# Batched 64x64 matmul: a second quarter of the last four a tiles loaded as fp32 on ScalarE's queue

## Chip, cores and metric

The kernel runs on one core of a Trainium2 chip. The metric is the device time of one execution in microseconds, as a median of runs. A core has five engines, each with its own queue of instructions: TensorE (PE; PEld is its weight load), VectorE (DVE), ScalarE (ACT), GpSimd (POOL) and SyncE (SP). DMAs are issued from the queues of SyncE, ScalarE and GpSimd, and all are carried by the same 16 DMA engines. In the profile q0 is GpSimd's DMA ring, q1 SyncE's and q10 ScalarE's.

## The reference

1024 independent products of 64x64 matrices in fp32:

```python
"a": np.random.randn(1024, 64, 64).astype(np.float32)
"b": np.random.randn(1024, 64, 64).astype(np.float32)

def reference(a, b):
    return np.matmul(a, b).astype(np.float32)
```

a and b are 16.8 MB each, and so is the output.

## The kernel before

**Tiling.** b and the output are cut into 16 tiles of 64 products (index t, 1 MB each), a into 8 tiles of 128 products (index s, 2 MB each); tile s of a serves t = 2s and 2s + 1. The multiplication is done in bf16: for each tile t TensorE runs 64 pairs of weight load and matmul, with a block-diagonal weight tile (`at_bd`) that holds transposed blocks of a, and `b_bf` as the moving data.

**a.** A tile of a is loaded in four quarters h = 0 to 3 of 512 KB (128 rows of 4 KB). For s = 1 to 7 `load_a` (line 70) has GpSimd load h = 0, 1, 2 with DMAs that cast from fp32 to bf16 on the way (256 KB written, tile `a_sb`), and SyncE load h = 3 as it is (fp32, tile `a_raw`). Tile 0 (`load_first_a`) is all fp32, two quarters from SyncE and two from ScalarE, each into a borrowed output buffer. Both tiles come from `a_pool`, three buffers each, so the load of tile s + 3 needs the buffer of tile s free. Load 4 is issued in the round t = 0, loads 5, 6 and 7 in the rounds t = 2, 4 and 6.

There are two ways from a to its transposed form `at_sb`. For s = 1, 2, 3 (`ON_DVE`) `transpose_dve` (line 116) has ScalarE cast h = 3 to bf16 (line 126) and VectorE transpose each quarter (line 128). For s = 0 and s = 4 to 7 `regroup` (line 100) brings the quarters into one tile `a_bf` in the order v, h, k on VectorE: line 109 copies the three cast quarters, line 112 casts and copies the fourth; then `transpose` (line 133) lets TensorE transpose and ScalarE copy the result from PSUM (line 141). `spread` (lines 154 and 164, VectorE) puts `at_sb` into the block-diagonal tile, of which there are two.

**b.** `load_b` (line 94) loads tile t as fp32, 512 rows of 2 KB, from SyncE where t is even and from ScalarE where t is odd. Three buffers: b(t + 3) is issued when the cast of b(t) has freed its buffer. `cast` (line 173) turns it into bf16 on VectorE (tile 0 on ScalarE; the last tile is shared by both, lines 178 and 180).

**Output.** `multiply` (line 187) runs the matmuls in two halves, each evacuated from PSUM in four copies (line 206). ScalarE does them all up to t = 6; from then on VectorE takes two of the last four in odd t. The stores of t = 0 to 13 are issued by GpSimd, 1 MB each, one round after the tile (`HOLD`), and those of the last two tiles by SyncE and ScalarE in halves and quarters (line 195).

**Order.** The order of the calls in the main loop is each engine's order (`manual_schedule`). In a round t: spread(t+1) and cast(t+1), load_b(t+3), load_a where it is due, the second half of a transposition, multiply(t), then the work on a for s + 2, and the store of t - 1. A DMA issue that waits holds up what stands behind it on its queue. On ScalarE that is the evacuation of tile t, on GpSimd the next store.

Of the kernel before, what the change touches and what calls it, by code (L numbers as in the profile page):

```python
# [8 lines left out]
fp32 = mybir.dt.float32  # L9
bf16 = mybir.dt.bfloat16  # L10
# [3 lines left out]
def kernel(  # L14
# [14 lines left out]
    nc = tc.nc  # L29
# [7 lines left out]
    N_BD = 2  # L37
    HOLD = 2
    ON_DVE = (1, 2, 3)

    a_v = a.rearrange("(s g h) (mp v) k -> s h g mp (v k)", h=4, g=32, v=16)
    b_v = b.rearrange("(t g h) (kp u) n -> t (h kp) g (u n)", h=4, g=16, u=2)
# [3 lines left out]
    a_pool = ctx.enter_context(tc.tile_pool(name="a_pool", bufs=A_AHEAD))  # L46
# [15 lines left out]
    a_tiles, b_tiles, abf_tiles, at_tiles, bbf_tiles = {}, {}, {}, {}, {}  # L62
# [6 lines left out]

    def load_a(s):  # L70

        a_sb = a_pool.tile([128, 3, 16, 64], bf16, name="a_sb")
        for h in range(3):
            nc.gpsimd.dma_start(  # L74
                out=a_sb[:, h, :, :].rearrange("p v k -> p (v k)"), in_=a_v[s, h], single_packet=True
            )
        a_raw = a_pool.tile([128, 16, 64], fp32, name="a_raw")
        nc.sync.dma_start(out=a_raw[:].rearrange("p v k -> p (v k)"), in_=a_v[s, 3])
        a_tiles[s] = a_sb, a_raw

    def load_first_a():

# [17 lines left out]
    def regroup(s):  # L100
        a_sb = a_tiles.pop(s)
        a_bf = work.tile([128, 16, 4, 64], bf16, name="a_bf")
        if s == 0:
            for h in range(4):
                copy = nc.scalar.copy if h % 2 else nc.vector.tensor_copy
                copy(a_bf[:, :, h, :], a_sb[h].rearrange("p (v k) -> p v k", v=16))  # L106
        else:
            cast_sb, raw = a_sb
            nc.vector.tensor_copy(  # L109
                a_bf[:, :, 0:3, :], cast_sb[:].rearrange("p h v k -> p v h k")  # L110
            )
            nc.vector.tensor_copy(a_bf[:, :, 3, :], raw[:])  # L112
        abf_tiles[s] = a_bf
        at_tiles[s] = work.tile([128, 32, 4, 4, 4], fp32, name="at_sb")

    def transpose_dve(s, half):
        cast_sb, raw = a_tiles[s]
        if half == 0:
            at_tiles[s] = work.tile([128, 4, 8, 4, 4, 4], fp32, name="at_sb")
        for h in (2 * half, 2 * half + 1):  # L120
            rows = cast_sb[:, h, :, :] if h < 3 else None
            if h == 3:
                rows = work.tile([128, 16, 4, 64], bf16, name="a_bf")[:, 0:4, :, :].rearrange(
                    "p x y k -> p (x y) k"
                )
                nc.scalar.copy(rows, raw[:])  # L126
            pairs = rows.rearrange("p v k -> p (v k)").bitcast(fp32)
            nc.vector.transpose(  # L128
                at_tiles[s][:, h].rearrange("p g w mp vo -> p w vo g mp"),
                pairs.rearrange("p (vo w kp) -> p w vo kp", vo=4, w=4),  # L130
            )

    def transpose(s, j):
        a_cols = abf_tiles[s][:].rearrange("p v h k -> p v (h k)").bitcast(fp32)
        for wl in range(2):
            at_ps = t_psum.tile([128, 4, 128], fp32, name="at_ps")
            for vo in range(4):
                nc.tensor.transpose(  # L138
                    at_ps[:, vo, :], a_cols[:, 4 * vo + 2 * j + wl, :], identity[:]
                )  # L140
            nc.scalar.copy(  # L141
                at_tiles[s][:, :, 2 * j + wl, :, :],
                at_ps[:].rearrange("p vo (g mp) -> p g mp vo", mp=4),
            )

    def spread(t):
        bd = bd_tiles[t % N_BD]
        at_sb = at_tiles[t // 2]
        for h in range(4):
            rows = slice(32 * h, 32 * h + 32)  # L150
            if t // 2 in ON_DVE:
                for i in range(2):
# [34 lines left out]
    def multiply(t):  # L187
# [20 lines left out]
        for half in range(2):  # L208
# [19 lines left out]
            if not last:  # L228
                copies = [nc.scalar.copy] * 4
                if half and t % 2 and t > 2 * max(ON_DVE):  # L230
                    copies[2:] = [nc.vector.tensor_copy] * 2
# [7 lines left out]
    with tc.manual_schedule():  # L239
# [7 lines left out]
        make_identity(nc, identity)  # L247
        nc.gpsimd.memset(bd_tiles[1][:, 0:8], 0.0)
        load_a(1)
        load_b(2)  # L250
        nc.gpsimd.memset(bd_tiles[1][:, 8:16], 0.0)
        load_a(2)
        regroup(0)
        transpose(0, 0)
        transpose(0, 1)
        spread(0)
        cast(0)
        for t in range(n_t):
            s, half = t // 2, t % 2
            if t + 1 < n_t:  # L260
                spread(t + 1)
                cast(t + 1)
            if t + B_AHEAD < n_t:
                load_b(t + B_AHEAD)
            if half == 0 and 0 < s < n_s - 1 - A_AHEAD:
                load_a(s + 1 + A_AHEAD)
            if half == 0 and 0 < s < n_s - 1 and s + 1 not in ON_DVE:
                transpose(s + 1, 1)
            multiply(t)
            if t == 0:  # L270
                transpose_dve(1, 0)
                transpose_dve(1, 1)
                a_tiles.pop(1)
                load_a(A_AHEAD)
                load_a(A_AHEAD + 1)
            if t and s + 2 in ON_DVE and (half or s):
                for part in [0, 1] if t == 1 else [half]:
                    transpose_dve(s + 2, part)
                if half:
                    a_tiles.pop(s + 2)  # L280
            elif half == 0 and 0 < s and s + 2 < n_s:
                regroup(s + 2)
            elif half == 1 and s + 2 < n_s:
                transpose(s + 2, 0)
            if t >= HOLD - 1:
                store(t - HOLD + 1)
# [32 lines left out]
```

## Time and profile before

| what | value |
|---|---|
| median of 3 runs | 133.84 us (133.62 to 133.94) |
| profiled execution | 133.61 us |
| its span, first to last instruction | 131.8 us |
| DVE busy | 101.8 us (77%) |
| ACT busy | 88.1 us (67%) |
| PE busy | 59.6 us (45%) |
| POOL busy | 31.9 us (24%) |
| granted TensorE clock | 0.763 |
| casting quarter of a (GpSimd), issue to landing | 15.9 us, median of 21 |
| fp32 quarter of a (SyncE), issue to landing | 17.3 us, median of 7 |
| VectorE waiting for b, whole span | 4.9 us in 3 waits, the longest 2.0 |

The profile is one execution. Busy time is what an engine spent in instructions other than issuing DMAs; a share of the span says nothing yet about what limits the end, since another engine's work or a transfer may have ended last at each step. The chain of waits follows the last instruction back through what released it. The DMA view counts packets and bytes of each ring and the time that the packets took as a share of 16 engines; a casting load's bytes are counted as written, half of what was read.

### The profile page before, as it was taken

What the parts mean: (1) busy time and instruction counts of PE and PEld (TensorE: products, weight loads), DVE (VectorE), ACT (ScalarE), POOL (GpSimd) and SP (SyncE); (2) the same over time, 40 slices, a digit from 0 to 9 for tenths busy, and PEclk for the clock granted to TensorE, in tenths of its full rate; (3) what the DMA queues carried; (4) which work ended last, traced back from release to release, by engine and by line L of the source; (5) the groups of instructions that cost most, each with busy time, mean ns of one, the idle gap of its engine ahead of it and who ended that gap; (6) DMA issues with size and microseconds to landing.
All of it is one profiled execution on the core that took longest, in us unless ns stands there. A gap on an engine that the chain in (4) does not pass through costs nothing.

```text
span 131.8 us, 2750 instructions
## 1 busy us (share of the span) xinstructions
PE 59.6 (45%) x1104; PEld 56.7 (43%) x1104; DVE 101.8 (77%) x144; ACT 88.1 (67%) x158; POOL 31.9 (24%) x43
## 2 busy tenths in 40 slices
PE   0006405730550640908662883299369619465000
PEld 0006305730550630908552872298368618464000
DVE  5930399529999984999999998699999997898300
ACT  2125414999495096492999989469969996549920
POOL 8991000340054000618031204300420302040000
PEclk9999975798568555595999599558968975579855
DMA  3999999999999999999999999999999999999993
GB/s 68 372 334 313 306 313 280 280 311 321 327 299 400 362 306 297 393 393 400 321 285 357 403 395 362 308 299 385 395 391 393 390 390 397 399 395 406 390 383 136
DMA packets 19020, 44.99 MB, mean 341 GB/s; under 512 B 1088, under 2 KB 3136, under 8 KB 19008
## 3 DMA queue, kind: packets, MB, share of 16 engines
q0 software_dynamic: 6832, 20.19, 50.6%
q1 hardware_dynamic: 7120, 14.68, 30.7%
q10 hardware_dynamic: 5056, 9.96, 20.1%
q8 instruction: 8, 0.13, 0.4%
q14 instruction: 4, 0.03, 0.1%
HBM read 33.55 MB, written 16.78 MB: 382 GB/s over the span
## 4 chain that ended last, share of the span: by engine, by line
DMA 53%; ACT 15%; DVE 14%; PE 6%; issue 5%; SPq 2%; ACTq 0%; DVEq 0%
DMA b_sb<-in_b_dram 53%; ACT o_sb L206 12%; PE o_ps L218 6%; DVE at_bd L164 4%; DVE b_bf L173 4%; DVE at_bd L154 2%; ACT b_bf L173 1%; DVE at_sb L128 1%; DVE o_sb L206 1%; DVE a_bf L109 1%; SPq L91 1%; ACT a_bf L126 1%; SPq L97 1%; ACT b_bf L180 1%; DVE a_bf L112 0%
## 5 line engine op out<-in xcount | busy, mean ns | idle before, releaser
L206 ACT COPY o_sb<-o_ps 64x512 f32<-64x512 f32 x112 | 65.0, 581 | 17.9 <-PE o_ps L218 13.5
L218 PEld LDWEIGHTS <-at_bd 128*128 128x128 bf16 x1024 | 45.2, 117 | 52.6 <-DVE b_bf L173 40.5
L218 PE MATMUL o_ps<-b_bf,at_bd 128*128 128x64 bf16 x960 | 45.6, 223 | 48.7 <-DVE b_bf L173 35.0
L164 DVE COPY at_bd<-at_sb 32x1024 f32<-32x1024 f32 x40 | 29.6, 739 | 6.6 <-ACT at_sb L141 5.6
L195 POOL DMA_DIRECT2D out_dram<-o_sb x14 | 15.4, 1103 | 46.1 <-ACT at_sb L141 20.6
L154 DVE COPY at_bd<-at_sb 32x512 f32<-32x512 f32 x48 | 22.0, 457 | 1.1
L74 POOL DMA_DIRECT2D a_sb<-in_a_dram x21 | 12.4, 606 | 38.5 <-DVE at_sb L128 33.2
L173 DVE CAST b_bf<-b_sb 128x2048 bf16<-128x2048 f32 x14 | 17.2, 1227 | 5.2 <-DMA b_sb<-in_b_dram 4.9
L138 PE MATMUL at_ps<-identity,a_bf 128*128 128x128 f32 x80 | 12.9, 329 | 11.0 <-ACT a_bf L106 11.0
L138 PEld LDWEIGHTS at_ps<-identity,a_bf 128*128 128x128 f32 x80 | 11.7, 176 | 11.0 <-issue 11.0
L141 ACT COPY at_sb<-at_ps 128x512 f32<-128x512 f32 x20 | 10.8, 591 | 2.7 <-PE at_ps L138 2.0
L128 DVE STREAM_TRANSPOSE at_sb<-a_sb 128x512 f32<-128x512 f32 x9 | 8.9, 1065 | 0.0
L128 DVE STREAM_TRANSPOSE at_sb<-a_bf 128x512 f32<-128x512 f32 x3 | 3.1, 1049 | 4.0 <-ACT a_bf L126 4.0
L206 DVE COPY o_sb<-o_ps 64x512 f32<-64x512 f32 x8 | 5.5, 690 | 0.2
L106 ACT CAST a_bf<-o_sb 128x1024 bf16<-128x1024 f32 x2 | 2.1, 1045 | 5.0 <-DMA o_sb<-in_a_dram 5.0
L173 ACT CAST b_bf<-b_sb 128x2048 bf16<-128x2048 f32 x1 | 1.9, 1897 | 4.0 <-DMA b_sb<-in_b_dram 4.0
L126 ACT CAST a_bf<-a_raw 128x1024 bf16<-128x1024 f32 x3 | 3.1, 1046 | 1.7 <-DMA a_raw<-in_a_dram 1.7
L109 DVE COPY a_bf<-a_sb 128x3072 bf16<-128x3072 bf16 x4 | 4.2, 1045 | 0.0
L106 DVE CAST a_bf<-o_sb 128x1024 bf16<-128x1024 f32 x2 | 2.8, 1383 | 1.8 <-DMA o_sb<-in_a_dram 1.8
L246 DVE MEMSET at_bd<- 128x4096 f32 x1 | 3.5, 3472 | 0.8 <-issue 0.8
L206 DVE COPY o_sb<-at_ps 64x256 f32<-64x256 f32 x8 | 3.4, 422 | 0.5 <-PE at_ps L218 0.4
L180 ACT CAST b_bf<-b_sb 128x512 bf16<-128x512 f32 x2 | 1.1, 616 | 3.5 <-DMA b_sb<-in_b_dram 3.5
(16 smaller groups left out, 15.4 us busy)
## 6 DMA issues: line engine op xcount, KB each, us to landing
out_dram<-o_sb POOLq DMA_DIRECT2D x14, 1024.0 KB, 22.7
a_sb<-in_a_dram POOLq DMA_DIRECT2D x21, 256.0 KB, 15.9
a_raw<-in_a_dram SPq DMA_DIRECT2D x7, 512.0 KB, 17.3
o_sb<-in_a_dram SPq DMA_DIRECT2D x2, 512.0 KB, 5.9
o_sb<-in_a_dram ACTq DMA_DIRECT2D x2, 512.0 KB, 7.0
out_dram<-o_sb SPq DMA_DIRECT2D x2, 512.0 KB, 5.5
out_dram<-o_sb SPq DMA_DIRECT2D x2, 256.0 KB, 5.2
out_dram<-o_sb ACTq DMA_DIRECT2D x2, 256.0 KB, 4.7
```

What stands on the lines that cost most here:

```text
L74: nc.gpsimd.dma_start(out=a_sb[:, h, :, :].rearrange("p v k -> p (v k)"), in_=a_v[s, h], single_packet=True)
L106: copy(a_bf[:, :, h, :], a_sb[h].rearrange("p (v k) -> p v k", v=16))
L109: nc.vector.tensor_copy(a_bf[:, :, 0:3, :], cast_sb[:].rearrange("p h v k -> p v h k"))
L128: nc.vector.transpose(at_tiles[s][:, h].rearrange("p g w mp vo -> p w vo g mp"), pairs.rearrange("p (vo w kp) -> p w vo kp", vo=4, w=4),)
L138: nc.tensor.transpose(at_ps[:, vo, :], a_cols[:, 4 * vo + 2 * j + wl, :], identity[:])
L141: nc.scalar.copy(at_tiles[s][:, :, 2 * j + wl, :, :], at_ps[:].rearrange("p vo (g mp) -> p g mp vo", mp=4),)
L154: nc.vector.tensor_copy(bd[rows, 8 * i : 8 * i + 8, :, h, :, :].rearrange("p g w mp vo -> p (g w) (mp vo)"), at_sb[block : block + 32, h]. ...
L164: nc.vector.tensor_copy(bd[rows, :, :, h, :, :].rearrange("p g w mp vo -> p (g w) (mp vo)"), at_sb[rows, half].rearrange("p g w mp vo -> p ...
L173: (nc.vector.tensor_copy if t else nc.scalar.copy)(b_bf[:], b_sb[:])
L195: store_queue(t, lo).dma_start(out=o_v[t, :, lo : lo + n, :], in_=o_sb[:, lo : lo + n].rearrange("p gh j wl n -> p (gh j wl n)"),)
L206: copies[2 * par + wl](dst, src)
L218: nc.tensor.matmul(o_ps[:, gl, g % 2, j, :], at_bd[:, j, g, :, u], b_bf[:, g, 64 * u : 64 * u + 64], start=(u == 0), stop=(u == 1),)
```

## The change

`load_a` takes one tile of 12 KB per partition, `room`, in which the cast quarters stand first and the fp32 quarters behind them, so both kinds now share one buffer and come free together. For s = 4, 5, 6, 7 (`TWO_RAW`) GpSimd casts two quarters instead of three, and h = 2 is loaded as fp32 by ScalarE; h = 3 stays with SyncE. `regroup` then copies two quarters and casts two on VectorE. For s = 1, 2, 3 the same quarters are loaded on the same queues as before.

```diff
+    TWO_RAW = (4, 5, 6, 7)
...
-        a_sb = a_pool.tile([128, 3, 16, 64], bf16, name="a_sb")
-        for h in range(3):
-            nc.gpsimd.dma_start(
-                out=a_sb[:, h, :, :].rearrange("p v k -> p (v k)"), in_=a_v[s, h], single_packet=True
-            )
-        a_raw = a_pool.tile([128, 16, 64], fp32, name="a_raw")
-        nc.sync.dma_start(out=a_raw[:].rearrange("p v k -> p (v k)"), in_=a_v[s, 3])
-        a_tiles[s] = a_sb, a_raw
+        n_cast = 2 if s in TWO_RAW else 3
+        room = a_pool.tile([128, 6144], bf16, name="a_sb")
+        a_sb = room[:, 0 : 1024 * n_cast].rearrange("p (h x) -> p h x", h=n_cast)
+        raw = room[:, 1024 * n_cast : 1024 * n_cast + 2048 * (4 - n_cast)].bitcast(fp32)
+        raw = raw.rearrange("p (h x) -> p h x", h=4 - n_cast)
+        for h in range(n_cast):
+            nc.gpsimd.dma_start(out=a_sb[:, h, :], in_=a_v[s, h], single_packet=True)
+        for h in range(n_cast, 4):
+            (nc.sync if h == 3 else nc.scalar).dma_start(out=raw[:, h - n_cast, :], in_=a_v[s, h])
+        a_tiles[s] = (
+            a_sb.rearrange("p h (v k) -> p h v k", v=16),
+            raw.rearrange("p h (v k) -> p h v k", v=16),
+        )
...
             cast_sb, raw = a_sb
+            n_cast = 2 if s in TWO_RAW else 3
             nc.vector.tensor_copy(
-                a_bf[:, :, 0:3, :], cast_sb[:].rearrange("p h v k -> p v h k")
-            )
-            nc.vector.tensor_copy(a_bf[:, :, 3, :], raw[:])
+                a_bf[:, :, 0:n_cast, :], cast_sb.rearrange("p h v k -> p v h k")
+            )
+            nc.vector.tensor_copy(
+                a_bf[:, :, n_cast:4, :], raw.rearrange("p h v k -> p v h k")
+            )
...
-                nc.scalar.copy(rows, raw[:])
+                nc.scalar.copy(rows, raw[:, 0])
```

## The prediction

> **What bounds the kernel now.** I read the page's slices and DMA queues first, then the DMA queues window by window, then the chain of waits, then VectorE's and ScalarE's timelines.
>
> The page's slices (tenths of busy DMA engines) and its queues: q0 is GpSimd's ring, which carries the casting loads of a and the stores of t = 0 to 13; q1 is SyncE's and q10 ScalarE's.
>
> ```profile
> DMA  3999999999999999999999999999999999999993
> q0 software_dynamic: 6832, 20.19, 50.6%
> q1 hardware_dynamic: 7120, 14.68, 30.7%
> q10 hardware_dynamic: 5056, 9.96, 20.1%
> HBM read 33.55 MB, written 16.78 MB: 382 GB/s over the span
> ```
>
> The 16 DMA engines are full from slice 2 to slice 39, and the shares sum to 101%. So an edit that leaves the bytes read and written as they are can win only what the engines don't fill now. At the end that is little: in the table by stretches the DMA share is 1.08 in 126 to 128 us, 0.86 in 128 to 130 and 0.08 in 130 to 131.8, about 0.8 us of full work missing.
>
> How the rings share the engines is seen in three windows of the DMA queue view (packets, MB, share of 16 engines): 40 to 44 us, 51 to 56 us, and 32 to 38 us.
>
> ```profile
> q0 software_dynamic: 196, 0.78, 50.6%
> q10 hardware_dynamic: 196, 0.40, 26.8%
> q1 hardware_dynamic: 198, 0.41, 26.4%
> ```
> ```profile
> q0 software_dynamic: 336, 1.05, 66.4%
> q1 hardware_dynamic: 331, 0.72, 38.9%
> q10 hardware_dynamic: 1, 0.00, 0.0%
> ```
> ```profile
> q0 software_dynamic: 282, 0.51, 45.1%
> q1 hardware_dynamic: 279, 1.02, 44.7%
> q10 hardware_dynamic: 213, 0.40, 17.8%
> ```
>
> Each ring with work gets one packet in turn, whatever its size. With three rings SyncE's gets 198 packets in 4 us (50 per us); with ScalarE's ring empty it gets 331 in 5 us (66 per us). ScalarE's ring is empty in gaps: 37 to 39.5, 51 to 56.5, 67.5 to 70.5, 93 to 94.5 us in the trace's packet record, because an odd b is issued only when a buffer comes free and its first packet follows some 4 us later (issued 52.54, first packet 56.5; 66.47 and 70.5). SyncE's ring is not empty once between 39 and 86 us.
>
> The chain of waits (start, us, what) says what the rest hangs on:
>
> ```profile
> 66.47 17.10 DMA b_sb<-in_b_dram
> ...
> 102.47 14.73 DMA b_sb<-in_b_dram
> ```
>
> b(t+3) is issued when cast(t) has freed its buffer, and takes some 16 us. By the landing records b8, b9, b10, b11, b12, b13, b14 land at 75.4, 83.6, 88.9, 93.2, 100.4, 106.6, 112.4 us; VectorE's casts of them start at 76.25, 83.66, 89.51, 95.31, 101.16, 106.97, 112.50. Only b11 has more than 0.9 us to spare. A ring that is slower by a microsecond is felt by VectorE at once.
>
> **What the change does, part by part.**
>
> DMA work: four quarters of 512 KB read, 128 packets each, go from casting to plain. In the third window q0 moves only casts (0.451 x 96 us / 282 = 153 ns a packet) and q1 almost only plain 4 KB loads (0.447 x 96 / 279 = 154 ns). 512 packets x 1 ns / 16 is nothing. Bounds: single packet records read 159 to 176 ns for a plain 4 KB load and 172 for a cast, so -0.4 to +0.1 us. I take 0.
>
> Which ring carries them: q0 keeps its turn whether it has a cast or a store to send, so taking casts out of it speeds no b. ScalarE's ring gains 8 packets on each engine per quarter, each between two turns of the others. Where it fills a gap of that ring, SyncE's ring loses 8 x 0.154 = 1.2 us; where it stands ahead of an odd b, that b also waits 8 turns of 0.154 + 0.165 + 0.086 = 0.4 us, 3.2 us, and SyncE loses only 8 x (0.154 - 0.086) = 0.5.
> - s = 4 (issued about 29.6, behind b3) falls into the gap at 37: SyncE loses 1.2. But its casts and store 0 are issued later (below), which thins q0 about as much. I take 0, bounds 0 and 1.2.
> - s = 5 (issued about 38, behind b5) falls into the gap at 51: b6, a6 and b8 on SyncE later by 1.2.
> - s = 6 (issued about 54, behind b7) falls into the gap at 67.5: another 1.2. b8 would land at 77.8 against a cast at 76.25.
> - s = 7 (issued about 67, behind b9) has no gap behind it: SyncE loses 0.5, b11 is 3.2 later, 96.4.
> b10 on SyncE's ring carries all three: 88.9 + 1.2 + 1.2 + 0.5 = 91.8 against a cast at 89.51. VectorE is 2.3 us late there. b11 at 96.4 is then in time (95.31 + 2.3).
>
> VectorE: four regroups. The copy falls from 128x3072 to 128x2048 bf16, the cast grows from 128x1024 to 128x2048:
>
> ```profile
> L173 DVE CAST b_bf<-b_sb 128x2048 bf16<-128x2048 f32 x14 | 17.2, 1227 | 5.2 <-DMA b_sb<-in_b_dram 4.9
> L109 DVE COPY a_bf<-a_sb 128x3072 bf16<-128x3072 bf16 x4 | 4.2, 1045 | 0.0
> L112 DVE CAST a_bf<-a_raw 128x1024 bf16<-128x1024 f32 x4 | 3.1, 775 | 0.0
> ```
>
> The copy costs between two thirds of the median 0.954 (0.64) and 0.954; I take 0.67. The cast costs between 1.23 (L173, same count and types) and 2 x 1.05 (the slowest L112); I take 1.23. Undisturbed before: 0.95 + 0.69; after: 1.90; +0.26 each, +1.0 in all, bounds 0.9 and 5. Those of s = 4, 5 and 6 (59.6, 71.5, 84.8 us) lie ahead of VectorE's waits for b8 and b10 and vanish in them; that of s = 7 (96.45) adds its 0.26. So b15, issued when cast(12) is done, is 2.3 + 0.26 = 2.6 us late.
>
> ScalarE's queue: four issues of 0.7 us (ACTq row of L97). The timeline (start, us, what, idle before) shows the cover:
>
> ```profile
> 36.51 4.74 ACT L206 COPY o_sb<-o_ps 64x512 f32<-64x512 f32 x8
> 45.91 4.74 ACT L206 COPY o_sb<-o_ps 64x512 f32<-64x512 f32 x8 [4.66 <-PE o_ps L218]
> 54.43 4.74 ACT L206 COPY o_sb<-o_ps 64x512 f32<-64x512 f32 x8 [1.92 <-PE o_ps L218]
> ```
>
> The room is one tile now, so each issue waits for VectorE's transposes and ScalarE's own copy. s = 4: 28.9 to 29.6, the eight evacuations of t = 1 behind it 0.7 later, inside the 1.70 idle before 35.36. s = 5: VectorE's third transpose ends at 37.4, so the evacuations of t = 2 start at 38.1 instead of 36.5; 1.6, inside the 4.66. s = 6: 53.45 + 0.7 = 54.15, before 54.43. s = 7: 0.7 at 67, inside the 2.91 idle before 86.92. Nothing is charged; without cover it is 0.7 + 1.6 + 0 + 0.7 = 3.0. GpSimd: a4's casts move from 25.2 to 28.9 and store 0 from 28.1 to about 30; a4 landed by 42.3 for a regroup at 59.6, so they are covered. SyncE's a6 moves from 51.74 to 53.5, behind b6, which is still loading.
>
> The tail: before, b15 lands at 117.2, and the last store is issued at 126.27 and lands 4.7 us later, behind others. 2.6 us later there is less left to store: q0's stores have moved on meanwhile. The last store then takes between 3.0 (1.3 from issue to first packet and 1.0 from last packet to landing, as the first a load has them, and 0.7 for 256 KB at 390 GB/s) and 4.7. The end moves by 2.6 - 1.7 = 0.9 to 2.6; I take 1.9, nearer the upper end since the stores of t = 14 and 15 still queue behind each other.
>
> Sum on the profiled execution: 133.61 (span 131.8 and 1.8 around it) + 1.9 = 135.5. It lies 0.2 below the median of the runs shown, 133.84, so the forecast is **135.7**.
>
> The Trainium skill ("DMA: Bandwidth & Descriptors", section "Issuing engines are not separate DMA queues") says that DMAs of all queues run on the same 16 engines, and that another issuing engine saves only the sequencer's issue time. By it the moved quarters change nothing, 133.8. The window rows agree with the first half; the turns, 66 packets per us against 50, show that a ring of one's own does decide whose packets go first.
>
> **The rivals.**
> - Nothing moves: the late b loads find slack, and the full DMA engines end when they did. For it: slices of 9, equal packet prices. Against it: 0.6 to 0.9 us of slack at b8 and b10 against 2.4 and 2.9 us. 133.8. That is the skill's case above.
> - Faster, through q0: four casts less are 512 x 0.153 / 16 = 4.9 us of its work, so stores run ahead, and q0 goes dry before b15 is in; b15 and the last stores then have the engines alone. It decides if q0 is dry before 117 us. From 117 to 122 us q0 is alone with over 100% of the engines, so some 8 us of stores stand there. For it: the work removed nearly reaches that. Against it: ScalarE's ring takes the same bytes first. It can win only the 0.8 us unfilled: 133.0.
> - Only VectorE's longer regroups are felt, the rings not: 1.0 us, less the 0.5 of s = 4 and 5, which vanish in VectorE's 1.63 idle before 83.66: 134.3.
> - ScalarE's waits aren't covered, since evacuations feed stores and PSUM: part of the 3.0 us on top, 137.0.
>
> **How the numbers follow.** Forecast 0.52, nothing 0.07, faster 0.12, VectorE alone 0.14, ScalarE on top 0.15. A difference of 0.2% (0.27 us) is about what a measurement of this kernel can tell from none. Slower: 0.52 + 0.14 + 0.15 = 0.81; within: 0.07; faster: 0.12. The range runs from 133.3, leaving out most of the faster case, to 137.5 (b15 late by 4, with the 1.2 of s = 4 and uncovered ScalarE, at a full tail). The slower cases alone span 134.2 to 137.5.
>
> **What would show it.** Right: b8 and b10 landing 2 to 3 us later and VectorE waiting for them; ScalarE's ring without gaps at 51 and 67 us and SyncE's at 50 packets per us there; the q0 share lower; b15 landing near 120; the last stores landing faster than 4.7 us. Wrong: b8 and b10 landing as before, VectorE's waits for b unchanged, new ScalarE waits on VectorE followed by late matmuls, or an end of the DMA engines before 130 us.

## The result and the profile after

The changed kernel takes 137.44 us (median of 4 runs, 137.0 to 137.53) against 133.89 us beside it (133.62 to 134.2): a ratio of 1.0262, 95% interval 1.0241 to 1.0283, or 3.5 us more. The forecast was 135.7, 1.9 us more. Its profiled execution has 137.53 us and a span of 135.4.

The page of the changed kernel, slices and queues:

```profile
DMA  3999999999999999999999999999999999997693
GB/s 68 375 329 312 305 312 278 282 312 373 335 324 403 344 319 389 396 395 346 310 402 385 402 359 320 381 392 394 395 388 396 390 392 376 398 356 276 230 336 130
q0 software_dynamic: 6256, 19.14, 45.5%
q1 hardware_dynamic: 7120, 14.68, 30.1%
q10 hardware_dynamic: 5632, 12.06, 23.4%
```

576 packets have gone from q0 to q10 (512 of data and some for semaphores). The engines were full to slice 39; now slices 37 and 38 are not, and the GB/s row has 276 and 230 there. The DMA engines ran out of work because the last stores came late.

How the rings shared the engines from 68 to 71 us (packets, MB, share), first before, then after:

```profile
q0 software_dynamic: 206, 0.47, 65.1%
q1 hardware_dynamic: 211, 0.43, 40.6%
q10 hardware_dynamic: 13, 0.02, 2.1%
```
```profile
q0 software_dynamic: 128, 0.48, 41.4%
q10 hardware_dynamic: 128, 0.48, 40.0%
q1 hardware_dynamic: 127, 0.26, 22.6%
```

This is the gap of ScalarE's ring that the prediction pointed at. Before, SyncE's ring got 211 packets of b8 through in it. After, the quarter of s = 6 takes a turn for each of SyncE's, at 4 KB a turn, and SyncE gets 127. From 51 to 54 us, with the quarter of s = 5, it is 199 against 134.

VectorE's timeline after (start, us, what, idle before), from cast(7)'s regroup to cast(9), and cast(14):

```profile
72.37 0.69 DVE L116 COPY a_bf<-a_sb 128x2048 bf16<-128x2048 bf16 x1
72.97 1.22 DVE L119 CAST a_bf<-a_sb 128x2048 bf16<-128x2048 f32 x1
75.63 2.83 DVE L173 COPY at_bd<-at_sb 32x1024 f32<-32x1024 f32 x4 [1.44 <-ACT at_sb L150]
79.56 1.23 DVE L182 CAST b_bf<-b_sb 128x2048 bf16<-128x2048 f32 x1 [1.10 <-DMA b_sb<-in_b_dram]
83.84 1.39 DVE L215 COPY o_sb<-o_ps 64x512 f32<-64x512 f32 x2 [3.05 <-ACT o_sb L215]
...
88.38 1.23 DVE L182 CAST b_bf<-b_sb 128x2048 bf16<-128x2048 f32 x1
...
117.31 1.23 DVE L182 CAST b_bf<-b_sb 128x2048 bf16<-128x2048 f32 x1 [0.76 <-DMA b_sb<-in_b_dram]
```

The regroup is as priced (0.69 + 1.22). The cast of b8 starts at 79.56 instead of 76.25, and that of b9 at 88.38 instead of 83.66; from there VectorE is some 5 us late to the end. But two of the four waits here are for ScalarE, which the prediction didn't have, and they are the longer ones. Over the whole span VectorE waits 3.5 us for b, against 4.9 before. ScalarE's timeline after shows where its delay comes from (ACTq rows are issues of DMAs):

```profile
38.41 3.40 ACTq L81 DMA_DIRECT2D a_sb<-in_a_dram  x1
41.85 9.50 ACT L215 COPY o_sb<-o_ps 64x512 f32<-64x512 f32 x16 [5.88 <-issue]
...
54.09 4.17 ACTq L81 DMA_DIRECT2D a_sb<-in_a_dram  x1
58.31 9.51 ACT L215 COPY o_sb<-o_ps 64x512 f32<-64x512 f32 x16 [5.21 <-DVE at_bd L163]
...
68.23 6.25 ACTq L81 DMA_DIRECT2D a_sb<-in_a_dram  x1
...
74.53 1.07 ACT L150 COPY at_sb<-at_ps 128x512 f32<-128x512 f32 x2 [5.61 <-issue]
```

An issue that was priced at 0.7 us holds ScalarE's queue for 3.40, 4.17 and 6.25 us, 0.1 to 2 us behind the issue of an odd b load, and everything behind it stands still. So after the result there were three theories: **ring** (the quarter takes turns from the b loads, as forecast), **hold** (ScalarE's queue stands still) and **VectorE** (the longer regroups).

The tail, by stretches, before and after. A row has the stretch and its length in us, the busy time of PE, PEld, DVE, ACT and POOL (with the number of instructions), the granted clock, the DMA share and GB/s:

```profile
120.00:123.00 3.00, 0.38 (x14) 0.26 (x9) 2.88 (x7) 2.93 (x6) 0.00 (x0) 1.00 1.01 401
123.00:126.00 3.00, 0.00 (x0) 0.00 (x0) 0.00 (x0) 2.88 (x9) 0.00 (x0) 0.67 1.05 387
```
```profile
120.00:123.00 3.00, 1.77 (x32) 1.64 (x32) 2.88 (x5) 1.21 (x3) 0.89 (x1) 0.59 0.64 244
123.00:126.00 3.00, 2.39 (x46) 2.40 (x46) 1.77 (x5) 2.93 (x6) 0.00 (x0) 0.50 0.98 344
126.00:129.00 3.00, 1.20 (x23) 1.04 (x20) 2.90 (x7) 2.92 (x7) 0.00 (x0) 0.77 0.64 218
```

In each of the two stretches at a share of 0.64 about 1.1 us of full work (3 x 0.36) is missing; before, the engines are full from 120 to 126.

### The profile page after: what moved, and what is told of

Its sections match the earlier page's. It is cut to its first block, busy times and chain, and to the rows that moved or that the text cites. A ratio compares the mean times of both kernels' runs of the same rounds, so it can differ in the third digit from the quotient of the medians.

```text
span 135.4 us, 2768 instructions
## 1 busy us (share of the span) xinstructions
PE 62.7 (46%) x1104; PEld 59.6 (44%) x1104; DVE 102.9 (76%) x144; ACT 88.1 (65%) x158; POOL 28.4 (21%) x39
## 4 chain that ended last, share of the span: by engine, by line
DMA 39%; DVE 21%; ACT 18%; PE 9%; issue 8%; SPq 2%; ACTq 0%; DVEq 0%
DMA b_sb<-in_b_dram 39%; ACT o_sb L215 14%; PE o_ps L227 8%; DVE b_bf L182 5%; DVE at_bd L173 5%; DVE at_bd L163 5%; DVE o_sb L215 2%; ACT b_bf L182 1%; DVE at_sb L137 1%; ACT at_sb L150 1%; SPq L97 1%; DVE a_bf L119 1%; ACT a_bf L135 1%; SPq L103 1%; PE at_ps L147 1%
## 5 line engine op out<-in xcount | busy, mean ns | idle before, releaser
L227 PEld LDWEIGHTS <-at_bd 128*128 128x128 bf16 x1024 | 47.6, 120 | 56.3 <-DVE b_bf L182 36.1
L227 PE MATMUL o_ps<-b_bf,at_bd 128*128 128x64 bf16 x960 | 46.7, 224 | 51.9 <-DVE b_bf L182 27.5
L204 POOL DMA_DIRECT2D out_dram<-o_sb x14 | 14.6, 1046 | 59.7 <-ACT o_sb L215 37.5
L163 DVE COPY at_bd<-at_sb 32x512 f32<-32x512 f32 x48 | 22.8, 476 | 1.1
L147 PE MATMUL at_ps<-identity,a_bf 128*128 128x128 f32 x80 | 13.5, 340 | 11.2 <-ACT a_bf L112 11.2
L147 PEld LDWEIGHTS at_ps<-identity,a_bf 128*128 128x128 f32 x80 | 12.4, 184 | 11.1 <-issue 11.1
L79 POOL DMA_DIRECT2D a_sb<-in_a_dram x17 | 9.8, 589 | 33.6 <-ACT a_bf L135 17.6
L119 DVE CAST a_bf<-a_sb 128x2048 bf16<-128x2048 f32 x4 | 4.9, 1221 | 0.0
L227 PE MATMUL at_ps<-b_bf,at_bd 128*128 128x64 bf16 x64 | 3.6, 242 | 1.4 <-DVE at_bd L173 1.4
L135 ACT CAST a_bf<-a_sb 128x1024 bf16<-128x1024 f32 x3 | 3.1, 1046 | 0.1
```

The source lines that it names most:

```text
L79: nc.gpsimd.dma_start(out=a_sb[:, h, :], in_=a_v[s, h], single_packet=True)
L119: nc.vector.tensor_copy(a_bf[:, :, n_cast:4, :], raw.rearrange("p h v k -> p v h k"))
L147: nc.tensor.transpose(at_ps[:, vo, :], a_cols[:, 4 * vo + 2 * j + wl, :], identity[:])
L163: nc.vector.tensor_copy(bd[rows, 8 * i : 8 * i + 8, :, h, :, :].rearrange("p g w mp vo -> p (g w) (mp vo)"), at_sb[block : block + 32, h]. ...
L204: store_queue(t, lo).dma_start(out=o_v[t, :, lo : lo + n, :], in_=o_sb[:, lo : lo + n].rearrange("p gh j wl n -> p (gh j wl n)"),)
L227: nc.tensor.matmul(o_ps[:, gl, g % 2, j, :], at_bd[:, j, g, :, u], b_bf[:, g, 64 * u : 64 * u + 64], start=(u == 0), stop=(u == 1),)
```

## The experiments

Times are medians beside the kernel before on the same chip, whose median was 133.46 for the first four, 133.51 for the next four and 134.05 for the last four; the ratios compare across them.

**The added quarter on GpSimd (e1_pool).**

```diff
-            (nc.sync if h == 3 else nc.scalar).dma_start(...)
+            (nc.sync if h == 3 else nc.gpsimd).dma_start(...)
```

> The changed kernel, but the added fp32 quarter is issued by GpSimd, so it stays in q0; VectorE's longer regroups stay. Hold theory (ScalarE's instruction queue stands still while its load of a waits for room behind a b load; that is where the 3.6 us come from): 133.6 to 134.3. Ring theory (a quarter in a hardware ring takes turns from the b loads): 133.6 to 134.3 as well. VectorE theory (the longer casts): 134.4 to 135.2, about 1 us over before.

134.97 us, ratio 1.0123 (1.0103 to 1.0143). The casts of b8 and b14 start at 75.97 and 112.70 (before: 76.25 and 112.50). So without the move to another ring the b loads come in time, and some 2 us of the loss are gone; but 1.5 us remain, where the VectorE theory had its figure.

**Both fp32 quarters on SyncE (e2_sync).**

```diff
-            (nc.sync if h == 3 else nc.scalar).dma_start(...)
+            nc.sync.dma_start(...)
```

> The changed kernel, but both fp32 quarters are issued by SyncE. ScalarE's queue holds no load of a. Hold theory: 134.0 to 135.5, most of the 3.6 us gone. Ring theory: 137.5 to 139, since every even b now stands behind two quarters in SyncE's ring, 8 turns of 0.4 us each. VectorE theory: as with GpSimd, 134.4 to 135.2.

140.26 us, 1.0522 (1.0493 to 1.0552): the ring theory's side, and beyond its figure. VectorE's longest waits in this run (us in total, times, longest):

```profile
DVE b_bf L182 <- DMA b_sb<-in_b_dram: 12.3, 4, 4.5
DVE at_bd L173 <- ACT at_sb L150: 5.9, 1, 5.9
```

12.3 us of waiting for b, against 4.9 before, 4.47 of them ahead of b8 and 3.84 ahead of b10, both of SyncE's ring. ScalarE's queue holds no load of a here, so the hold theory can't make this time.

**ScalarE's issue behind the evacuations (e3_late).**

```diff
-            (nc.sync if h == 3 else nc.scalar).dma_start(...)
+            if h == 3:
+                nc.sync.dma_start(out=raw[:, h - n_cast, :], in_=a_v[s, h])
+            else:
+                late.append((raw[:, h - n_cast, :], a_v[s, h]))
...
+    def load_late():
+        while late:
+            dst, src = late.pop()
+            nc.scalar.dma_start(out=dst, in_=src)
...
             multiply(t)
+            load_late()
```

> The changed kernel, but ScalarE issues its quarter of a at the end of the round, behind the evacuations of multiply(t), and not ahead of them. The ring carries the same packets in nearly the same order. Hold theory: 134.0 to 135.2. Ring theory: 135.7 to 137.4, as the changed kernel or little less.

136.91 us, 1.0258 (1.0243 to 1.0274), the same as the changed kernel. VectorE's timeline in it:

```profile
79.13 1.23 DVE L191 CAST b_bf<-b_sb 128x2048 bf16<-128x2048 f32 x1 [3.12 <-DMA b_sb<-in_b_dram]
...
84.94 1.23 DVE L191 CAST b_bf<-b_sb 128x2048 bf16<-128x2048 f32 x1
...
93.14 1.23 DVE L191 CAST b_bf<-b_sb 128x2048 bf16<-128x2048 f32 x1 [2.12 <-DMA b_sb<-in_b_dram]
```

The two waits for ScalarE around 75 and 84 us are gone, and b8 and b10, the loads that the prediction named, are what VectorE waits for now, 2.9 and 3.6 us later than before. ScalarE's queue is still held by these issues, for 3.30, 0.97 and 2.98 us, but behind the evacuations of the round, where VectorE doesn't wait for it. In the changed kernel the waits for ScalarE stood in front of the waits for b; without them the late b loads cost the same.

**ScalarE held, loads as before (e7_hold).**

```diff
                 load_a(s + 1 + A_AHEAD)
+                for _ in range({1: 2, 2: 2, 3: 3}[s]):
+                    nc.scalar.copy(idle_to[:], idle_sb[:])
```

> The kernel before, all its loads unchanged, with copies of a scratch tile added to ScalarE's queue where the changed kernel has its load of a: two of 1.9 us in the rounds t = 2 and t = 4, three in t = 6 (3.8, 3.8 and 5.7 us against issues of 3.40, 4.17 and 6.25 us). Hold theory: 136.0 to 137.5. Ring and VectorE theory: 133.6 to 134.5, since ScalarE has idle time.

133.85 us, 1.0032 (1.0018 to 1.0047). The chain does get late: cast(9) starts at 85.63, and the last store is issued at 128.09 instead of 126.27. But the end moves by 0.4 us: the DMA engines stay full, and 1.4 of the 1.8 us disappear in the tail. So the hold alone does not make the loss, and without VectorE's waits for ScalarE (e3_late) the loss stays: the hold theory falls.

**The common buffer alone (e4_room).**

```diff
-    TWO_RAW = (4, 5, 6, 7)
+    TWO_RAW = ()
```

> The changed kernel with no second fp32 quarter (TWO_RAW empty): only the common buffer of cast and fp32 quarters is left of the change. Ring theory: no quarter moves, 133.2 to 133.8, as before; a4's casts are issued some 4 us later (25.2 to 28.9) and are still 17 us early. If the common buffer is what cost 1.5 us in the run with the quarter on GpSimd: 134.5 to 135.2.

134.16 us, 1.0045 (1.0027 to 1.0063), between the two figures. a4's casts go out later, GpSimd's ring stays empty for some 2 us near 32 us, and the b loads use it: cast(4) starts at 50.05 instead of 51.23, and the last store is issued 1.2 us earlier. That the end is nevertheless 0.6 later isn't explained by these runs.

**VectorE's longer regroups alone (e9_vector).**

```diff
-                a_bf[:, :, 0:3, :], cast_sb[:].rearrange("p h v k -> p v h k")
+                a_bf[:, :, 0:2, :], cast_sb[:, 0:2].rearrange("p h v k -> p v h k")
...
-            nc.vector.tensor_copy(a_bf[:, :, 3, :], raw[:])
+            nc.vector.tensor_copy(
+                a_bf[:, :, 2:4, :], stand_in[:].rearrange("p h v k -> p v h k"))
```

> The loads of before, unchanged, with VectorE's regroups of s = 4 to 7 as long as the changed kernel's: a copy of two quarters, and a cast of 128x2048 fp32 that reads a tile of zeros (quarters 2 and 3 are left out of the result). VectorE theory for the 1.5 us of the GpSimd run: 134.5 to 135.2. DMA theory (a plain 4 KB packet keeps the engines longer than a cast of 4 KB): 133.3 to 133.9.

133.70 us, 1.0015 (0.9998 to 1.0033). The VectorE theory falls. Of the 1.2% of the GpSimd run, the buffer has 0.45 and the regroups 0.15; some 0.6% (0.8 us) is left, as a difference of three ratios that are each uncertain by 0.2. What it is isn't shown. Plain packets in place of casts in q0 were not tried alone, and the packets' own time speaks against them as the main cause: summed over the run it is 134.7 us of 16 engines in the GpSimd run, 134.6 with the common buffer alone and 134.5 before.

**Four casts (e10_cast4).**

```diff
+    ALL_CAST = (4, 5, 6, 7)
+        n_cast = 4 if s in ALL_CAST else 3
...
-        for h in range(3):
+        for h in range(n_cast):
...
+        if n_cast == 3:
+            nc.sync.dma_start(out=a_raw[:].rearrange("p v k -> p (v k)"), in_=a_v[s, 3])
```

> The change the other way round: for s = 4 to 7 all four quarters are cast by GpSimd's DMAs, none is loaded by SyncE, and VectorE regroups in one copy of 128x4096 bf16 (about 1.25 us against 1.64). Ring theory: SyncE's ring loses 8 packets per engine and tile, so the even b loads land earlier and VectorE no longer waits for b8; the end is held by the full DMA engines: 132.6 to 133.4. If plain packets cost the engines more than casts, another 1 us less: 131.8 to 132.6. Hold theory: as before, 133.2 to 133.7.

134.23 us, 1.0052 (1.0034 to 1.0071): no gain. The mechanism went as the ring theory says: cast(8) starts at 73.18 without a wait, the last store is issued at 123.62 instead of 126.27. The price did not: here an earlier chain is worth nothing, since the DMA engines are full to the end anyway. The 131.8 to 132.6 expected for dearer plain packets did not come either. The stretches at its end:

```profile
121.00:124.00 3.00, 0.00 (x0) 0.00 (x0) 0.51 (x2) 2.50 (x7) 0.00 (x0) 0.50 1.02 387
124.00:127.00 3.00, 0.00 (x0) 0.00 (x0) 0.00 (x0) 0.00 (x0) 0.00 (x0) 0.50 1.04 365
127.00:130.00 3.00, 0.00 (x0) 0.00 (x0) 0.00 (x0) 0.00 (x0) 0.00 (x0) 0.50 0.98 331
```

From 124 us on no engine but the DMA engines works, and these are full to 130. Why it is 0.5% slower than before is open.

**The one fp32 quarter on ScalarE instead of SyncE (e5_swap).**

```diff
-        nc.sync.dma_start(out=a_raw[:]...
+        (nc.scalar if s > 3 else nc.sync).dma_start(out=a_raw[:]...
```

> The kernel before, with the one fp32 quarter of s = 4 to 7 issued by ScalarE in place of SyncE. Bytes, casts and VectorE's work are as before; ScalarE's queue holds the issue as in the changed kernel. Ring theory: SyncE's ring loses what ScalarE's gains and the gaps of ScalarE's ring take it, so b8 and b10 are no later: 133.0 to 134.2. Hold theory: 136 to 137.5.

133.97 us, 1.0032 (1.0017 to 1.0047). The hold is there (cast(9) at 85.77, VectorE waits 4.1 us in one piece for ScalarE's evacuation), and costs as little as in e7_hold. VectorE waits for b only once, 1.61 us ahead of b14. So one fp32 quarter costs little in either of the two rings with the b loads; the loss comes when these rings carry one more.

**Four buffers for b (e11_after_b4, e12_before_b4),** in the changed kernel and in the one before:

```diff
-    B_AHEAD = 3
+    B_AHEAD = 4
...
+            if t == 0:
+                load_b(3)
```

> The changed kernel with four buffers for b instead of three, so each b load from b3 on is issued one round earlier (about 6 us). Ring theory with the closed loop (a b that lands late holds up the cast that frees the buffer for the next): b8 and b10, some 4 us late in the changed kernel, are in time again, and 133.8 to 134.8 is left, near the kernel with the common buffer alone. If the loss sits elsewhere (VectorE, ScalarE's queue, the tail): 136.5 to 137.5.

> The kernel before with four buffers for b. Its DMA engines are short of only 0.8 us of work at the end: 132.7 to 133.7 by the ring theory, no more to win than that. If b's lateness held the end of the kernel before too: 130 to 132.5.

135.76 us, 1.0139 (1.0107 to 1.0171), and 135.08 us, 1.0086 (1.0058 to 1.0114). Both miss their figures, since a fourth buffer costs 1.0 us by itself: in e12_before_b4 the last store is issued 2.9 us earlier (123.33), yet its DMA engines are busy to 131.7. Why the same bytes take them longer there is open. Between the two the change costs 0.7 us instead of 3.5, and in the changed kernel the last store is issued at 127.35 instead of 130.74. But other than expected, b8 and b10 are not in time again: they land at 77.35 and 92.23 us against 74.61 and 87.71 in e12_before_b4, VectorE waits 6.6 us for b (2.6 there), and the last store is still issued 4.0 us later. The last landings are at 131.8 and 132.1 all the same. So the late b loads remain; with the whole chain begun earlier, nearly all of their delay lies in time in which the DMA engines have work anyway. The run does not show that a b in hand keeps a late b from delaying the chain.

**Fewer tiles (e13_six, e14_fivesix).**

```diff
-    TWO_RAW = (4, 5, 6, 7)
+    TWO_RAW = (6,)
...
+    TWO_RAW = (5, 6)
```

> The changed kernel with a second fp32 quarter for s = 6 alone. Ring theory: its packets fill the gap of ScalarE's ring near 68 us, b8 comes about 2 us later, of which 0.9 was to spare; the late 1 to 1.5 us are within what the tail takes up: 134.0 to 134.7, close to the 134.2 of the common buffer alone. If the loss is in proportion to the quarters moved (VectorE, DMA work): 135.0.

> The changed kernel with second fp32 quarters for s = 5 and 6. Ring theory: the delays on SyncE's ring add up, b8 about 3 us late, past what the tail takes up (1 to 1.5): 135.0 to 136.2. In proportion to the quarters moved: 135.8.

134.46 us, 1.0034 (1.0014 to 1.0054), and 134.88 us, 1.0074 (1.0052 to 1.0096). One quarter costs no more than the buffer alone. For two the ring figure was too high: cast(8) starts at 77.22 after a wait of 2.11 for b8, but the last store is issued only 0.6 us later than before (126.88), which the tail takes up: it lands at 130.86, before at 130.91. The 0.7 us by which the span of that execution is longer lie behind the last landing. Four quarters cost 2.6%, so the loss isn't in proportion to the quarters moved. It fits a chain that may be late for free at first and pays from there; but the quarters of s = 4 and 7 were not tried alone, and they may cost more than those of 5 and 6.

## Why the prediction was right, and where it was short

**The mechanism was right, though the changed kernel's own trace shows only part of it.** Losing turns to the moved quarters, SyncE's ring brings b8 and b10 some 4 us late in the changed kernel (79.5 and 92.9 us); the forecast was 2.4 and 2.9. VectorE's waiting for them, the sign that the prediction named, is seen there only ahead of b8 (1.1 us); the other long waits there are for ScalarE, which the prediction did not foresee. It is e3_late that shows the forecast chain whole: the two waits for ScalarE are gone, VectorE waits 7.4 us for b, 5.2 of them ahead of b8 and b10, and the time is the same. From there the late casts issue the next b loads late (b15 at 107.72 instead of 102.47 in the changed kernel), and the tail gives some back. Where the quarters were placed is where they went: in e3_late's packet records they pass through ScalarE's ring at 35 to 41, 49 to 55, 67 to 71 and 81 to 85 us.

The case by which another issuing engine saves only issue time (the Trainium skill, "DMA: Bandwidth & Descriptors", section "Issuing engines are not separate DMA queues") would have given 133.8. The runs show the same quarters at 1.0123 in GpSimd's ring, 1.0258 and 1.0262 in ScalarE's and 1.0522 in SyncE's. The Trainium skill, same page, section "Queues, rings and completion order", has each DMA engine serve its rings in turn, packet by packet; with 128, 128 and 127 packets in one window, the trace agrees.

**How much of the loss is the ring's.** The quarter in ScalarE's ring (e3_late) and the quarter in GpSimd's differ by 1.9 us on the same chip. That much is shown to come from the ring. The 1.5 us that stay in GpSimd's ring have other causes (buffer 0.6, regroups 0.2, the rest open), and the prediction had only the regroups among them. Whether they all stand in the changed kernel's 3.5 us too, whose DMA engines are not full at the end, isn't shown.

**The term that was mis-sized is the lateness of b15**: forecast 2.6 us, measured 4.5 (last store issued at 130.74 instead of 126.27; b15 lands at 121.7 instead of 117.2). So the forecast's 1.9 us at the end became 3.5. That the range reached to 137.5 is partly luck: its upper end took b15 late by 4 us through the quarter of s = 4 and ScalarE's waits, with nothing given back in the tail. The two steps that were short are these.
- A quarter in a gap of ScalarE's ring was priced at 1.2 us, the time that its own packets take. The windows show 84 packets lost to SyncE's ring near 68 us and 65 near 51. If they are made up when three rings are active, at 50 a microsecond, that is 1.7 and 1.3 us, an estimate from these rows. In e3_late, without VectorE's waits for ScalarE, b8 lands at 79.0 (forecast 77.8, before 75.4) and b10 at 93.1 (forecast 91.8, before 88.9).
- ScalarE's issues were priced at 0.7 us each and took 3.40, 4.17 and 6.25. The row for it was there: in the trace of before, SyncE's issues of a_raw, behind its b loads, took a median of 5.2 us, and I took the row of the b issues instead. It makes the chain later (4.5 us against 3.8 in e3_late) but not the end: e3_late takes as long as the changed kernel. "Nothing is charged" held, though not for the reason given: of the cover (4.66, 1.92 and 2.91 us idle) nothing was left at the first two places and 0.99 us at the third.

**The tail** was right: forecast that the end moves by 0.0 to 1.7 us less than b15, with 0.7 taken; measured 4.5 against 3.6 in the span. The last store took 3.0 us to land (issued 130.74, landed 133.7), the lower bound of the forecast. But the parts of that bound differ: 1.7 us to the first packet, 0.9 for the packets and 0.4 from the last packet to the landing, against 1.3, 0.7 and 1.0. That their sum is the same is luck; the first a load, to which the prediction pointed, has 1.4 us ahead of its first packet and 0.3 behind its last. Of the 3.6, 2.8 lie ahead of the last landing (130.9 and 133.7) and 0.8 behind it. Of these 0.8, 0.5 lie at one closing instruction of GpSimd, which ends 0.67 us after the one before it instead of 0.16, and 0.2 at SyncE's closing waits. Why is open.

**VectorE** was right: 1.91 against 1.90 us for a regroup, and 0.15% in the end. **DMA work** was taken as unchanged, with +0.1 us as its upper bound; the packets' own time is 134.5 us of 16 engines before and 134.9 after, so 0.4 more. **The common buffer** was taken as nothing, with a4's later casts set off against a lost turn; it does bring b4 1.2 us earlier, but costs 0.45% at the end.

**The rivals.** "Nothing moves" and "faster" did not come; the four-cast run shows why nothing was to be won on that side. The price of "ScalarE on top", 137.0, is nearest to the time, but not its mechanism: with the issues moved behind the evacuations and VectorE's waits for ScalarE gone, the time stays.

## What to carry to other kernels

When the DMA engines are full, ask of each load not what it costs but which ring it stands in, and who else is in that ring and beside it: in these traces rings with work got equal numbers of packets, so a load moved into a quiet ring slowed the others, though the DMA engines did nearly the same work. A transfer nobody waits for belongs in the ring whose backlog nobody waits for. And here an early chain was worth nothing beyond the point where the DMA engines are full to the end, while a late one was nearly free up to the same point: find that point before pricing a stall.

## What the runs showed that was not expected

- A DMA issue can hold its engine's queue for microseconds: ScalarE's load of a took 0.59 us to issue where no b load had just been issued (29.53 us), and 3.40 to 6.25 where one had been issued up to 2 us before.
- An odd b load's first packet comes some 4 us after its issue (66.47 and 70.7; 52.54 and 56.5 in the kernel before), that of SyncE's first load of a 1.4 us (0.74 and 2.16), that of ScalarE's 3.4 (0.75 and 4.13). Most of the gaps of ScalarE's ring are these 4 us, since it has one load at a time. What sets them isn't shown.
- In e7_hold 13.4 us of added copies on ScalarE in the middle made the last store 1.8 us later and cost 0.4 us at the end, and a last store issued 2.7 or 2.9 us earlier (e10_cast4, e12_before_b4) made the kernel 0.5 and 0.9% slower.
